# Attention as one loop over the tiles of all heads, with scores two tiles further ahead and the product with v two steps behind its transposition

## The chip, the cores and the metric

The kernel runs on one core of one Trainium2 chip. The metric is the device time of one execution in microseconds (us). Engines are named as in the profile: PE is TensorE's matmul, PEld its weight load, DVE is VectorE, ACT is ScalarE, POOL is GpSimd, SP is SyncE, which here only issues DMAs.

## The reference

Two sequences of 512 tokens with 1024 features go through one encoder layer. What matters here is the attention half:

```python
q = rms_norm(q, q_norm); k = rms_norm(k, k_norm)          # 8 heads of 96 = 64 + 32 rotary
y_att = block_attention(q, k, v)                          # softmax(q k^T * scale) v, v: 64 per head
h = h + jnp.concatenate([y_pool, y_att], axis=-1) @ w_o
u2 = rms_norm(h, ln2)
h = h + (jax.nn.silu(u2 @ w_gate) * (u2 @ w_up)) @ w_down
gate = jax.nn.sigmoid(rms_norm(h, ple_norm) @ w_ple_gate)
return h + gate * (p @ w_ple_proj)
```

Attention is bidirectional, without a mask. All arithmetic is in fp32; the kernel keeps an operand of a product as a high and a low part and makes each product of three matmuls (`mm3`).

## The kernel before, in words

A sequence has 512 tokens, that is 4 tiles of 128 rows (`NT = 4`). There are two sequences (`s0`, `s1`) of 8 heads each, so the attention has 16 heads and 64 tiles. For each tile of a head three things are done:

- `scores(q, h, t)`: three matmuls into a PSUM bank tagged `s` (three such banks), the row maximum on DVE (L517), its product with the row's scale (L518, one element per row), the exponential on ACT with the row's sum (L520), the reciprocal (L521) and the division by the sum, on DVE for t = 2 (L523) and on POOL else (L525). The result p lies in an SBUF slot tagged `F` (12 of them, shared with the scratch of the projections).
- `turned(q, h, j)`: four 128x128 transposes on PE (L531), one from each of the head's four p tiles, into a bank tagged `pt` (two of them), and a split into a high part (ACT, L128) and a low part (DVE, L131) in a slot tagged `PT` (four of them). So no `turned` of a head can start before all four p tiles of the head are there.
- `values(q, h, j)`: two matmuls (L543) that add into the head's bank `y`. There is one such bank. After the head's fourth `values`, `head_out` empties it with ACT (L553) and DVE (L554).

The loop `attention` goes over the heads, and in a head over its four tiles. While a head is turned, the scores of the next head are issued, one tile for each tile turned, so scores stand four tiles ahead. `values` follows its `turned` by one step, and the last one of a head comes at once after its last `turned`.

Other work is woven in. `must` holds one generator for each group of four heads: the projection of the next four heads (q, k, v, rotary part, normalisation, and the transposition of q and k of each head, lines 441 to 505). `RATE` says how many pieces of it are issued for each tile (2, 2, 1, 1). The scores of a head need its q and k to be there, so `run(block)` issues all the rest at the fourth head of a group. Once the block is used up in the third group, pieces of `more` are issued: the output projection `output(s0)`, which first splits eight tiles of attention and pooling results (`mixed`, tiles `ys`) and then goes through eight column tiles of `w_o` (matmuls `o<-ys`, addition L608). `output(s1)` follows after the attention.

The order of the text is not the order on the engines. The program is built with `tile.TileContext(nc, schedule_with_timeline_sim=True)`: a planner fixes each engine's order before the program runs, and takes work that it believes ready ahead of earlier work that it believes blocked. On the chip each engine then follows that order.

```python
BUFS = {"A": 20, "QK": 8, "V": 4, "PT": 4, "W": 8, "R": 2, "F": 12, "G": 4}
PSUM_BUFS = {"s": 3, "y": 1, "pt": 2, "g": 2}
"soft": "ppdp",
RATE = (2, 2, 1, 1)
attention([project(s0, 1, w1), chain(features(s1), project(s1, 1, w1)), again(), iter(())], o0, early)
run(o0)
```

Of the kernel before, what the change touches and what calls it, by code (L numbers as in the profile page):

```python
# [11 lines left out]
F32 = mybir.dt.float32  # L12
# [6 lines left out]
T = 512  # L19
NT = T // P  # L20
# [4 lines left out]
PAD = 8  # L25
# [13 lines left out]
HG = 4  # L39
# [47 lines left out]
def hybrid_layer(ctx: ExitStack, tc: tile.TileContext, a: dict, out: bass.AP):  # L87
# [6 lines left out]
    def nm(s):  # L94
        serial[0] += 1
        return f"{s}{serial[0]}"

    def sbuf(s, tag, shape, dt):
        return pool.tile([P] + shape, dt, tag=tag, name=nm(s), bufs=BUFS[tag])

    def At(s, tag="A", dt=F32R):
        return sbuf(s, tag, [2, T], dt)

    def Ft(s):
        return sbuf(s, "F", [T], F32)
# [6 lines left out]
    def eng(name, i=0):  # L112

        return nc.gpsimd if TURNS[name][i % len(TURNS[name])] == "p" else nc.vector

    def Ps(s, tag=None):
        if tag is None:
            tag = ALL_BANKS[turn[0] * 3 % 8]
            turn[0] += 1
        return psum.tile([P, T], F32, tag=tag, name=nm(s), bufs=PSUM_BUFS[tag])  # L120

    def col(s, n=16, bufs=8):
        return pool.tile([P, n], F32, tag=f"c{n}", name=nm(s), bufs=bufs)

    def split(hi, lo, src, hi_eng="act", lo_eng=nc.vector):

        if hi_eng == "act":
            nc.scalar.activation(hi, src, AF.Copy)  # L128
        else:
            nc.vector.tensor_copy(hi, src)  # L130
        lo_eng.tensor_tensor(lo, src, hi.bitcast(F32), op=ALU.subtract)  # L131
# [21 lines left out]
    def mm3(ps, lhs, rhs, first, last, more=False):  # L153

        nc.tensor.matmul(ps, lhs[0], rhs[0], start=first, stop=False, skip_group_check=more)  # L155
        nc.tensor.matmul(ps, lhs[0], rhs[1], start=False, stop=False, skip_group_check=more)  # L156
        nc.tensor.matmul(ps, lhs[1], rhs[0], start=False, stop=last, skip_group_check=more)  # L157

    def act(t, sl=slice(0, T), rows=P):
        return t[:rows, 0, sl], t[:rows, 1, sl]  # L160
# [4 lines left out]
    def tok(t):  # L165
        return slice(t * P, (t + 1) * P)
# [74 lines left out]
    s0, s1 = seqs  # L241
# [269 lines left out]
    def scores(q, h, t):  # L511
        qT, kT, rq, _, hh = q.heads[h]
        ps = Ps("s", "s")
        mm3(ps, act(qT, tok(t), QK), act(kT, rows=QK), True, True)
        r = rq[:, t * HG + hh:t * HG + hh + 1]
        c = col("sm", 4, 12)
        nc.vector.tensor_reduce(c[:, 0:1], ps, axis=AX.X, op=ALU.max, negate=True)  # L517
        nc.vector.tensor_tensor(c[:, 1:2], c[:, 0:1], r, op=ALU.mult)  # L518
        p = Ft("p")
        nc.scalar.activation(p, ps, AF.Exp, scale=r, bias=c[:, 1:2], accum_out=c[:, 2:3])  # L520
        nc.vector.reciprocal(c[:, 3:4], c[:, 2:3])  # L521
        if eng("soft", t) is nc.vector:
            nc.vector.tensor_scalar(p, p, c[:, 3:4], None, op0=ALU.mult)  # L523
        else:
            nc.gpsimd.tensor_scalar(p, p, c[:, 3:4], 1.0, op0=ALU.mult, op1=ALU.mult)  # L525
        q.p[h].append(p)

    def turned(q, h, j):
        ps = Ps("pt", "pt")
        for t in range(NT):  # L530
            nc.tensor.transpose(ps[:, tok(t)], q.p[h][t][:, j * P:(j + 1) * P], ident)  # L531
        pt = At("pt", "PT")
        split(pt[:, 0, :], pt[:, 1, :], ps)
        q.pt[h].append(pt)

    def values(q, h, j):
        _, _, _, v, hh = q.heads[h]
        if j == 0:
            q.y[h] = Ps("y", "y")

        vv = v[j // 2][:, j % 2, hh].rearrange("p a d -> p (a d)")
        for i in range(2):
            nc.tensor.matmul(q.y[h], vv, q.pt[h][j][:, i, :], start=(j == 0 and i == 0), stop=(j == NT - 1 and i == 1))  # L543

    def head_out(q, h):
        if h % 4 == 0:
            q.ya4 = At("ya", dt=F32)
        y = q.ya4[:, h // 2 % 2, :]
        if h % 2 == 0:
            q.ya.append((NG + h // 2, y))  # L550
        o = h % 2 * VD
        f = Ft("yf")
        nc.scalar.activation(f[:VD, :], q.y[h][VD:, :], AF.Copy)  # L553
        nc.vector.tensor_tensor(y[o:o + VD, :], q.y[h][:VD, :], f[:VD, :], op=ALU.add)  # L554

    def attention(must, more, after):

        for q in seqs:
            q.p = {h: [] for h in range(H)}
            q.pt = {h: [] for h in range(H)}  # L560
            q.y, q.ya = {}, []
        heads = [(q, h) for q in seqs for h in q.order]
        for t in range(NT):
            scores(s0, 0, t)
        for n, (q, h) in enumerate(heads):
            block = must[n // HG]
            for i in range(NT):
                if h % HG == HG - 1 and i == 0:
                    run(block)
                if n + 1 < len(heads):  # L570
                    scores(*heads[n + 1], i)
                turned(q, h, i)
                if i:
                    values(q, h, i - 1)
                for _ in range(RATE[n // HG]):
                    if next(block, 0) is not None and n >= 2 * HG:
                        next(more, None)
            values(q, h, NT - 1)
            head_out(q, h)
            after(q, h)  # L580


    def mixed(q, i):
# [184 lines left out]
    def run(*gens):  # L768
        for g in gens:
            for _ in g:  # L770
                pass
# [14 lines left out]
    s0, s1 = seqs  # L786
# [2 lines left out]
            next(g, None)  # L789

    RATE = (2, 2, 1, 1)
    latents()
    pools = pooling()
    steps(pools, 1)
# [15 lines left out]
    def again():  # L810
        yield from project(s1, 0, head_weights(0))

    attention([project(s0, 1, w1), chain(features(s1), project(s1, 1, w1)), again(), iter(())], o0, early)
    run(o0)
    phase[0] = "raw2"
# [254 lines left out]
```

## Time and profile before

| | us |
|---|---|
| median of 3 runs (1205.45 to 1207.92) | 1206.1 |
| the profiled execution | 1203.58 |
| its span, from the first to the last instruction | 1201.6 |
| PE busy in the span | 1131.3 |
| DVE busy | 927.1 |
| ACT busy | 591.2 |
| POOL busy | 195.6 |

The profiled execution is one execution of its own; its span leaves out 2.0 us before the first and after the last instruction. Busy time is time in which an engine executes; PE's is modelled from the matmuls' sizes. The granted clock of PE is given as a share of its full speed. The attention lies between 155 us, where the first scores start, and 381 us, where the last head's result is written.

### The profile page before, as it was taken

To read this page: it belongs to the slowest core of one execution; us is meant where nothing else is said; L and a number is where in the kernel's file an instruction comes from. 1 tells how busy PE (TensorE), PEld (TensorE's weight loads), DVE (VectorE), ACT (ScalarE), POOL (GpSimd) and SP (SyncE) were. 2 spreads that over 40 slices of the span, in tenths; PEclk is the share of its full clock that TensorE was granted. 3 is DMA by queue.
4 is the path that set the end of the run, shared out by engine and by line. 5 is a ranking of instruction groups with operands and counts; after the bars stand their busy time and mean duration, and the time that the engine had idled before them with its cause. 6 is when DMAs were issued, how large, how long until landed. Compare 5 with 4: busy or idle time off the path is not lost.

```text
span 1201.6 us, 15110 instructions
## 1 busy us (share of the span) xinstructions
PE 1131.3 (94%) x5232; PEld 936.6 (78%) x5232; DVE 927.1 (77%) x1738; ACT 591.2 (49%) x1135; POOL 195.6 (16%) x191
## 2 busy tenths in 40 slices
PE   7999979897999989999999999999669999999897
PEld 7998757785888867888888888888558888887775
DVE  7387799999684789988776877768547776896798
ACT  7154478777563536555444545455212222345553
POOL 3543562755330310000000000000000000001200
PEclk9999999997999989999999999999979999999999
DMA  6211100111242521644425444356896675526036
GB/s 216 69 56 58 36 1 1 53 36 53 88 142 88 167 79 55 226 176 158 163 91 185 175 158 140 105 193 234 296 412 233 251 278 203 210 88 227 27 122 220
DMA packets 53644, 173.26 MB, mean 144 GB/s; under 512 B 6208, under 2 KB 6976, under 8 KB 53568
## 3 DMA queue, kind: packets, MB, share of 16 engines
q1 hardware_dynamic: 53568, 172.30, 41.2%
q8 instruction: 41, 0.67, 0.2%
q14 instruction: 35, 0.29, 0.1%
HBM read 119.33 MB, written 52.95 MB: 143 GB/s over the span
## 4 chain that ended last, share of the span: by engine, by line
PE 73%; DVE 15%; DMA 4%; ACT 3%; issue 2%; POOL 1%; SPq 1%; DVEq 0%; POOLq 0%; ACTq 0%
PE a L156 7%; PE a L157 7%; PE a L155 7%; PE b L156 5%; PE b L155 5%; PE b L157 5%; PE d L157 3%; PE d L155 3%; PE d L156 3%; PE o L155 2%; PE o L156 2%; PE o L157 2%; PE c L155 2%; PE c L157 2%; PE c L156 2%
## 5 line engine op out<-in xcount | busy, mean ns | idle before, releaser
L128 ACT ACTIVATE w<-s 128x512 fp32r<-128x512 f32 (+2 forms) x168 | 97.1, 579 | 170.2 <-PE b L157 63.2
L156 PE MATMUL a<-u,w 128*128 128x512 f32 x444 | 173.5, 391 | 0.2 <-POOL u L131 0.2
L155 PE MATMUL a<-u,w 128*128 128x512 f32 x444 | 171.3, 391 | 1.5 <-ACT w L128 0.8
L157 PE MATMUL a<-u,w 128*128 128x512 f32 x444 | 171.2, 391 | 0.7 <-DVE w L131 0.7
L128 ACT ACTIVATE w<-raw 128x512 fp32r<-128x512 f32 (+2 forms) x126 | 70.9, 578 | 156.5 <-PE a L157 96.2
L155 PE MATMUL b<-u,w 128*128 128x512 f32 x296 | 117.1, 397 | 19.5 <-DMA u<-opT 19.5
L185 POOL TENSOR_TENSOR r<-base,neghalf 128x4 f32<-128x4 f32 x6 | 6.9, 1149 | 714.8 <-DVE base L194 714.3
L131 DVE TENSOR_TENSOR w<-s,w 128x512 fp32r<-128x512 f32 (+2 forms) x168 | 105.0, 628 | 22.7 <-ACT w L128 22.0
L156 PE MATMUL b<-u,w 128*128 128x512 f32 x296 | 117.3, 397 | 4.0 <-DVE u L131 4.0
L157 PE MATMUL b<-u,w 128*128 128x512 f32 x296 | 117.3, 396 | 1.1 <-DVE w L131 1.1
L155 PEld LDWEIGHTS a<-u,w 128*128 128x128 f32 x444 | 83.7, 189 | 20.0 <-ACT u L128 1.5
L157 PEld LDWEIGHTS a<-u,w 128*128 128x128 f32 x444 | 83.7, 188 | 18.9 <-DVE w L131 1.5
L156 PEld LDWEIGHTS a<-u,w 128*128 128x128 f32 x444 | 83.7, 188 | 18.0 <-POOL u L131 0.7
L131 DVE TENSOR_TENSOR w<-raw,w 128x512 fp32r<-128x512 f32 (+2 forms) x126 | 79.4, 642 | 23.5 <-ACT w L128 23.5
L155 PEld LDWEIGHTS b<-u,w 128*128 128x128 f32 x296 | 56.8, 192 | 32.7 <-DMA u<-opT 19.9
L156 PEld LDWEIGHTS b<-u,w 128*128 128x128 f32 x296 | 56.6, 191 | 17.0 <-DVE u L131 5.3
L157 PEld LDWEIGHTS b<-u,w 128*128 128x128 f32 x296 | 56.7, 191 | 13.5 <-DVE w L131 1.8
L155 PE MATMUL c<-u,w 128*128 128x512 f32 x148 | 58.7, 400 | 4.9 <-DVE x L727 4.9
L926 DVE TENSOR_TENSOR h<-h,a 128x512 f32<-128x512 f32 x64 | 42.4, 687 | 26.1 <-PE a L157 23.3
L641 DVE TENSOR_TENSOR s<-raw 128x512 f32<-128x512 f32 (+2 forms) x42 | 26.4, 628 | 43.1 <-DMA raw<-in_w_down 15.2
L157 PE MATMUL c<-u,w 128*128 128x512 f32 x148 | 58.6, 396 | 0.0
L156 PE MATMUL c<-u,w 128*128 128x512 f32 x148 | 58.6, 396 | 0.0
(234 smaller groups left out, 2844.7 us busy)
## 6 DMA issues: line engine op xcount, KB each, us to landing
opT<-st SPq DMA_DIRECT2D x44, 512.0 KB, 4.5
u<-opT SPq DMA_DIRECT2D x44, 512.0 KB, 7.7
opB<-st SPq DMA_DIRECT2D x33, 512.0 KB, 3.7
u<-opB SPq DMA_DIRECT2D x33, 512.0 KB, 9.9
raw<-in_w_gate SPq DMA_DIRECT2D x24, 512.0 KB, 4.3
raw<-in_w_up SPq DMA_DIRECT2D x24, 512.0 KB, 3.6
raw<-in_w_down SPq DMA_DIRECT2D x24, 384.0 KB, 6.2
raw<-in_w_o SPq DMA_DIRECT2D x16, 512.0 KB, 3.6
```

The lines of the kernel that those rows point to most:

```text
L128: nc.scalar.activation(hi, src, AF.Copy)
L131: lo_eng.tensor_tensor(lo, src, hi.bitcast(F32), op=ALU.subtract)
L155: nc.tensor.matmul(ps, lhs[0], rhs[0], start=first, stop=False, skip_group_check=more)
L156: nc.tensor.matmul(ps, lhs[0], rhs[1], start=False, stop=False, skip_group_check=more)
L157: nc.tensor.matmul(ps, lhs[1], rhs[0], start=False, stop=last, skip_group_check=more)
L185: nc.gpsimd.tensor_tensor(r[:, :n], base, neghalf[:, :n], op=ALU.pow)
L641: eng("wadd", k).tensor_tensor(d, x, y, op=op)
L926: nc.vector.tensor_tensor(h, h, ps, op=ALU.add)
```

## The change

The two nested loops become one loop over 64 turns, and the scores are taken from a list of 64 tiles, also across the border of a head. Before the loop six tiles are scored (`NT + AHEAD_S`) in place of four; then one is scored in each turn. `values` follows its `turned` by two turns (`LAG_V`), also across the border of a head, and `head_out` and `after` follow the head's last `values`. The p tile of t = 3 lies in a slot tagged `G` (four of them, 528 elements) in place of `F`. If the next tile to be scored belongs to a head that has not been projected, the rest of the block is issued first; with six tiles ahead this comes at turn 10 of a group of 16 where it came at turn 12.

```diff
-        p = Ft("p")
+        p = sbuf("p", "G", [T + 2 * PAD], F32)[:, :T] if t == NT - 1 else Ft("p")
...
-        for t in range(NT):
-            scores(s0, 0, t)
-        for n, (q, h) in enumerate(heads):
-            block = must[n // HG]
-            for i in range(NT):
-                if h % HG == HG - 1 and i == 0:
-                    run(block)
-                if n + 1 < len(heads):
-                    scores(*heads[n + 1], i)
-                turned(q, h, i)
-                if i:
-                    values(q, h, i - 1)
-                for _ in range(RATE[n // HG]):
-                    if next(block, 0) is not None and n >= 2 * HG:
-                        next(more, None)
-            values(q, h, NT - 1)
-            head_out(q, h)
-            after(q, h)
+        tiles = [(q, h, t) for q, h in heads for t in range(NT)]
+        turns = [(q, h, j) for q, h in heads for j in range(NT)]
+        block = [None]
+
+        def more_scores():
+            if tiles:
+                if tiles[0][1] not in tiles[0][0].heads:
+                    run(block[0])
+                scores(*tiles.pop(0))
+
+        for _ in range(NT + AHEAD_S):
+            more_scores()
+        for n, (q, h, j) in enumerate(turns):
+            group = n // (NT * HG)
+            block[0] = must[group]
+            if h % HG == HG - 1 and j == 0:
+                run(block[0])
+            more_scores()
+            turned(q, h, j)
+            if n >= LAG_V:
+                values(*turns[n - LAG_V])
+                if turns[n - LAG_V][2] == NT - 1:
+                    head_out(*turns[n - LAG_V][:2])
+                    after(*turns[n - LAG_V][:2])
+            for _ in range(RATE[group]):
+                if next(block[0], 0) is not None and group >= 2:
+                    next(more, None)
+        for q, h, j in turns[-LAG_V:]:
+            values(q, h, j)
+        head_out(q, h)
+        after(q, h)
...
+    AHEAD_S, LAG_V = 2, 2
```

## Rows read from the trace of the kernel before

**Rows 1.** The page: its first line, the engines' busy time, and PE's granted clock in 40 equal slices of the span.

```profile
span 1201.6 us, 15110 instructions
PE 1131.3 (94%) x5232; PEld 936.6 (78%) x5232; DVE 927.1 (77%) x1738; ACT 591.2 (49%) x1135; POOL 195.6 (16%) x191
PEclk9999999997999989999999999999979999999999
```

**Rows 2.** Busy time of each engine (and its instructions) in three stretches: length, PE, PEld, DVE, ACT, POOL, granted clock, share of the DMA engines, GB/s.

```profile
155.00:298.00 143.00, 122.61 (x635) 96.97 (x636) 134.95 (x314) 109.52 (x239) 81.48 (x108) 0.94 0.11 30
298.00:381.00 83.00, 82.86 (x410) 68.12 (x409) 57.65 (x105) 46.22 (x85) 22.76 (x20) 1.00 0.33 108
381.00:400.00 19.00, 19.00 (x86) 15.73 (x85) 9.43 (x12) 7.38 (x10) 0.00 (x0) 1.00 0.45 144
```

**Rows 3.** What PE waited for between 155 and 298 us: line, releaser, total us, times, longest. These are all the rows of that answer.

```profile
PE qkt L503 <- DVE v L131: 6.9, 2, 4.3
PE s L155 <- ACT p L520: 6.1, 5, 2.9
PE y L543 <- DVE pt L131: 3.1, 5, 1.3
PE qkt L503 <- DVE qkT L136: 1.4, 2, 0.8
PE y L543 <- ACT pt L128: 1.2, 2, 0.6
PE pt L531 <- DVE pt L131: 0.7, 1, 0.7
PE qkt L503 <- DVE sm L518: 0.6, 2, 0.3
PE pt L531 <- DVE p L523: 0.5, 1, 0.5
```

**Rows 4.** The same for DVE between 155 and 298 us, the longest of its rows.

```profile
DVE ssqq L446 <- ACT sqq L445: 1.6, 3, 1.0
DVE sm L521 <- ACT p L520: 1.4, 5, 0.6
DVE ya L554 <- ACT yf L553: 1.3, 3, 0.6
```

**Rows 5.** Row maxima (L517, DVE, one for each tile scored) in three stretches; the count is behind the busy time.

```profile
155.00:168.60 13.60, 6.05 (x9) 1.00 0.00 1
168.60:207.00 38.40, 8.81 (x13) 1.00 0.00 1
207.00:262.30 55.30, 12.86 (x19) 0.97 0.11 29
```

**Rows 6.** Transposes of p (L531, PE and its weight loads, four for each tile turned) in the same stretches.

```profile
155.00:168.60 13.60, 1.59 (x8) 1.05 (x8) 1.00 0.00 1
168.60:207.00 38.40, 10.56 (x68) 8.59 (x69) 1.00 0.00 1
207.00:262.30 55.30, 9.63 (x60) 7.57 (x59) 0.97 0.11 29
```

**Rows 7.** Groups of instructions by line over the whole span: count, busy us, mean ns of one, idle time of the engine just before them and its releasers.

```profile
L520 ACT ACTIVATE p<-s,sm,rq 128x512 f32<-128x512 f32 x64 | 49.9, 780 | 15.3 <-DVE sm L518 15.0
L131 DVE TENSOR_TENSOR pt<-pt,pt 128x512 fp32r<-128x512 f32 x64 | 43.4, 681 | 4.6 <-ACT pt L128 4.5
L517 DVE TENSOR_REDUCE sm<-s 128x1 f32<-128x512 f32 x64 | 43.3, 681 | 2.8 <-PE s L157 2.4
L518 DVE TENSOR_TENSOR sm<-sm,rq 128x1 f32<-128x1 f32 x64 | 18.6, 294 | 0.2
L554 DVE TENSOR_TENSOR ya<-y,yf 64x512 f32<-64x512 f32 x16 | 10.9, 682 | 8.9 <-ACT yf L553 8.6
L553 ACT ACTIVATE yf<-y 64x512 f32<-64x512 f32 x16 | 9.5, 594 | 13.7 <-PE y L543 13.6
```

**Rows 8.** One line of the answer for the tile `sm`: durations of L518 in ns, shortest, median and longest, and the first and last start.

```profile
L518 DVE TENSOR_TENSOR sm<-sm,rq x64: 132/150/2091, 158.3 to 360.7; 128x1 f32<-128x1 f32 x64
```

**Rows 9.** Busy time of each engine in two short stretches, columns as in rows 2.

```profile
282.00:289.00 7.00, 2.58 (x7) 1.23 (x7) 7.00 (x12) 3.95 (x11) 3.99 (x3) 0.52 0.33 97
289.00:298.00 9.00, 8.35 (x32) 6.72 (x33) 8.44 (x22) 5.35 (x11) 4.50 (x5) 0.61 0.08 34
```

**Rows 10.** The chain that ended last, in order of time, between 286 and 300 us: start, us on the chain, what.

```profile
289.65 1.06 PE qkt L503 x4
...
291.14 0.43 PE s L156
...
291.99 0.85 PE y L543 x2
...
297.25 0.70 PE s L155 x3
...
298.18 0.44 PE pt L531 x4
```

**Rows 11.** Instructions of ACT and of POOL in order of time: start, us, what.

```profile
275.71 2.27 ACT L128 ACTIVATE ys<-yp 128x512 fp32r<-128x512 f32 x4
277.79 2.26 ACT L128 ACTIVATE ys<-ya 128x512 fp32r<-128x512 f32 x4
...
281.84 3.46 POOL L131 TENSOR_TENSOR ys<-ya,ys 128x512 fp32r<-128x512 f32 x2
```

## The prediction, made before the changed kernel ran

> **What bounds the kernel now.** I read the page first: PE is busy 94% of the span, DVE 77% [rows 1], so over the whole span this is a PE kernel. The change touches only the attention, so I then asked for busy times by stretch, and there the picture splits in two [rows 2]. From 155 to 298 us DVE is busy 134.95 of 143 us and PE 122.61: DVE is the bound and PE idles 20.4 us. From 298 to 400 us PE is busy 101.86 of 102 us and DVE 67.08: the output projection of the first sequence fills every gap of PE, and no order of instructions can gain anything there.
>
> The waits of PE in the first stretch say the same [rows 3]: PE waits for DVE results or for banks that DVE and ACT have not emptied. The two longest (4.3 and 2.9 us) lie together between 278 and 288 us. There PE is busy only 2.58 of 7 us while DVE is busy for all 7, and its clock falls to the lower level, 1.2 GHz: the granted clock is 0.52 and then 0.61 [rows 9]. Up to about 297 us the chain that ends last runs over PE at that level, with 0.43 us for a score matmul that takes 0.70 / 3 = 0.23 us afterwards [rows 10].
>
> So there are three sums that the change could touch: 8.05 us in which DVE idles in its own stretch (143 - 134.95), 20.4 us of idle PE in it, and the half-speed piece at its end.
>
> **What the change removes and adds.** No instruction: 64 scores, 256 transposes, 128 products with v, 16 emptied banks and the projections stay, with shapes as they are. The p tile of t = 3 in `G` has the same 128x512 elements, so 0 us; in return `F` holds at most 8 live p tiles as before (10 live ones less two in `G`). No DMA is added. Those that move are the loads for the output projection, which come two turns earlier; the second stretch has its DMA engines a third busy [rows 2], so they cost 0, and if that cover were gone the projection would start late in a stretch in which DVE is the bound anyhow.
>
> **What it moves: scores.** Each tile is scored two tiles earlier. The aim can only be that a head's four p tiles are ready when its first transposition comes. That run-ahead partly exists already: the planner does not keep the order of the text. By 168.6 us there are 9 row maxima and 8 transposes, that is 9 tiles scored and 2 turned; by 207 us 22 against 19; by 262.3 us 41 against 34 [rows 5, 6]. Scores thus stand 7, 3 and 7 tiles ahead, where the text says four or five. Where DVE is short of time, the lead shrinks; a higher place in the order does not make DVE faster, it only pushes something else back.
>
> What is pushed back can be priced. When the output projection may start (turn 10 of the third group, where it was turn 12), the same number of tiles has been scored, but two fewer have been turned and two or three fewer multiplied with v. DVE has then done 2 x 0.68 us of splits less [rows 7] and half an emptied bank, 0.34 us: 1.7 us. PE has 2 x 0.44 us of transposes [rows 10] and 2 x 0.46 us of products (two matmuls of 0.23) left over for the stretch in which it is the bound: 1.8 us. The stretch of DVE ends 1.7 us earlier and that of PE grows by 1.8 us: 0 within the reading.
>
> **What it moves: DVE's gaps.** The 8.05 us of idle DVE are waits for ACT's squares, for the exponential, for the emptying of `y` [rows 4]: short ones, in an order fixed beforehand, at places where the next tile's scores were not there yet. With two more tiles scored, DVE has independent row maxima to do in such gaps, unless one of the three `s` banks is missing. Bounds: 0 (a fixed order stays fixed, and the gaps only go elsewhere) to 8.05 us (all filled). I take a little under half, because some of the waits shown (the squares, 1.6 us) belong to the projection and not to the attention. That is the only term with a sign: -3.5 us.
>
> **What it moves: the product with v.** Two turns behind its transposition, PE does not wait for the low part that DVE writes; those waits are 3.1 + 1.2 us [rows 3]. In DVE's stretch PE's waits are covered by DVE, so they are worth 0 alone; if DVE were not the bound, 4.3 us would be the gain. What is late next is the one bank `y`. In the old text two turns lie between a head's last product and the next head's first; in the new one there is one.
>
> **Collisions.** L518 is a product of one element in each row. Its median is 0.150 us, its longest 2.091, its mean 0.294 [rows 7, 8]: 64 x 0.144 = 9.2 us go into stretched ones, and the long ones fall where POOL works. Nothing in the change alters how often this happens, only where: 0, with bounds of -9.2 (none left) and +9.2 us (twice as many). The Trainium skill, "SBUF — State Buffer", section "Who interferes with whom", says that a DVE instruction with two SBUF inputs and a POOL instruction that reads SBUF take a shared port one at a time, and that the order of issue decides who blocks; by that rule the trace agrees, and earlier scores would exchange some collisions for others.
>
> **Sum.** Added and removed 0, deferred work 0, DVE's gaps -3.5, the half-speed piece 0, collisions 0: the profiled execution of 1203.58 us would become 1200.1. The median of the runs is 1206.1, 2.5 us above that execution, and the same difference carried over gives 1202.6 us.
>
> **Rivals.**
>
> *Only the order on paper changes.* The planner already runs ahead by up to 7 tiles, DVE stays the bound with the same work, and its gaps move without closing. For it: the counts of rows 5 and 6, and the 0 of the deferred work. Against it: at 207 us the lead was down to three, less than a head. Time: 1206.1, within 0.2% (2.4 us, about what a measurement of this kernel can tell from no change).
>
> *The bank `y` stops PE (slower).* Emptying takes 0.594 us on ACT and 0.682 on DVE, and one more DVE instruction of 0.68 ahead of it: 1.96 us [rows 7]. One turn of PE is 0.70 + 0.44 = 1.14 us [rows 10]. So PE would be stopped 0.8 us at each of 15 head borders. In DVE's stretch that is hidden; in PE's stretch there are some four borders, 3.3 us, hence 1209.4 us; if it lay open at all fifteen, 12 us, 1218. It decides as soon as less than 0.8 us of other ready PE work stands between the two products. Against it: no wait of PE for L554 stands in rows 3, and an output projection lies beside these borders.
>
> *The stall at the end of DVE's stretch grows or comes twice (slower).* The splits `ys` for the output projection come in one burst, 4.5 us on ACT and 3.46 us on POOL for two of them [rows 11], while the last heads are projected. The three heads forced at turn 10 instead of one at turn 12 make this burst denser. One more such pause is 4.4 us of idle PE (7 - 2.58), of which some 4 us would reach the chain: 1210. The half-speed piece on the chain is 7.6 us (289.65 to 297.25), of which 3.8 are due to the clock. The Trainium skill, "TensorE: Matmul & The Clock Gate", section "HAM oscillation — how this bites in real kernels", states that PE's clock is throttled again after pauses, so that work after each pause starts at half speed; by that rule the trace agrees, and each further pause would cost again.
>
> *The stall goes away (faster than forecast).* PE has more score tiles done and one or two products in hand during the burst; if that keeps the clock up, 3.8 us more are gained: 1198.8.
>
> **How the numbers follow.** Chances: DVE's gaps half filled 0.34, the same with the stall gone 0.10, order on paper only 0.32, bank `y` 0.12, a larger stall or more collisions 0.12. Faster by over 0.2% (below 1203.7) is 0.34 + 0.10 = 0.44, the same 0.32, slower (above 1208.5) 0.24. The likeliest case's own range is 1200 to 1204, most of DVE's gaps to a third of them. The range for the time goes from 1196, all gaps filled (1206.1 - 8.05 = 1198) with part of the half-speed piece, to 1210, the larger stall and the bank's 3.3 us.
>
> **What would show it.** In the profile after: between 155 us and the end of DVE's stretch, DVE's idle time about 4 us instead of 8; the lead of scores over turned tiles two larger at 207 us; that stretch ends at about 294 us instead of 298; from there PE is full until 400. If the lead is not larger, the first rival holds. A wait of PE or its weight loads for L554 shows the bank. A granted clock below 1 at the end of the stretch shows that the stall stayed. I would be wrong if PE's full stretch had gaps, if the second half of the kernel, which is not touched, came out with another order, or if DVE's busy time itself changed by more than 3 us, since collisions would then decide.

## The result, and the profile after

The changed kernel takes 1214.69 us in the median of four runs (1213.45 to 1216.59), beside 1207.01 us for the kernel before (four runs, three of which gave the 1206.1 us known ahead of the prediction): a ratio of 1.0058, with a 95% interval of 1.0037 to 1.0079. It is slower, by 7.7 us between the medians and by 7.0 us by the ratio, where 1202.6 us and a gain had been predicted. The profiled execution is the slowest of the four, 1216.59 us.

The page of the changed kernel (its first line, busy times, granted clock in 40 slices), and two lines of each trace that frame the attention: the row maxima (first and last start behind the three durations) and the products of the output projection of the first sequence. After:

```profile
span 1214.8 us, 15098 instructions
PE 1135.0 (93%) x5232; PEld 937.3 (77%) x5232; DVE 924.4 (76%) x1738; ACT 589.8 (49%) x1135; POOL 198.0 (16%) x191
PEclk9999999988999998999999999999979999999999
```

```profile
L517 DVE TENSOR_REDUCE sm<-s x64: 660/678/693, 163.1 to 364.2; 128x1 f32<-128x512 f32 x64
```

```profile
L155 PE MATMUL o<-ys,wh x128: 388/390/791, 320.4 to 429.2; 128*128 128x512 f32 x128
```

Before:

```profile
L517 DVE TENSOR_REDUCE sm<-s x64: 661/678/692, 157.2 to 360.0; 128x1 f32<-128x512 f32 x64
```

```profile
L155 PE MATMUL o<-ys,wh x128: 387/390/791, 307.7 to 417.7; 128*128 128x512 f32 x128
```

The two spans differ by 13.2 us [rows 1], and these rows divide it. Up to the first row maximum the profiled execution of after lost 5.9 us (163.1 against 157.2); the change has not begun there, and the last section comes back to it. From the first row maximum to the last output product it lost 5.6 us (266.1 against 260.5). The rest of the kernel took 1.7 us more. Within the attention all of the loss lies ahead of the first output product, 157.3 us after the first row maximum instead of 150.5. From then on the two are alike: 108.8 and 110.0 us.

The three stretches of rows 2, moved by the 6 us by which the attention starts later (length, PE, PEld, DVE, ACT, POOL, granted clock, DMA share, GB/s):

```profile
161.00:304.00 143.00, 118.16 (x612) 93.11 (x613) 128.59 (x306) 106.22 (x234) 81.58 (x108) 0.94 0.10 30
304.00:387.00 83.00, 81.92 (x410) 67.26 (x409) 61.43 (x112) 48.59 (x89) 24.15 (x20) 1.00 0.32 102
387.00:406.00 19.00, 19.00 (x85) 15.76 (x84) 6.01 (x8) 5.50 (x8) 0.00 (x0) 1.00 0.35 111
```

In the same 143 us DVE idles 14.41 us, where it idled 8.05 [rows 2], and PE idles 24.8 where it idled 20.4. No engine has become clearly busier (POOL by 0.1 us). The stretch that DVE bounds is longer, and DVE stands still more often in it. What it waited for there (line, releaser, total us, times, longest):

```profile
DVE sm L521 <- ACT p L520: 5.6, 10, 1.6
DVE pt L131 <- ACT pt L128: 3.5, 2, 2.9
DVE sm L517 <- PE s L157: 2.4, 7, 0.5
DVE lat L136 <- ACT lat L135: 0.9, 2, 0.5
DVE ssqq L446 <- ACT sqq L445: 0.5, 2, 0.3
```

The first row was 1.4 us in five waits [rows 4], and two more were, before:

```profile
DVE sm L517 <- PE s L157: 1.0, 1, 1.0
DVE pt L131 <- ACT pt L128: 0.9, 3, 0.4
```

DVE's order now puts the reciprocal (L521) of a tile so near behind the same tile's maximum that the exponential is still running. One such place, in order of time on DVE (start, us, what, idle before it and releaser in brackets):

```profile
218.84 0.16 DVE L518 TENSOR_TENSOR sm<-sm,rq 128x1 f32<-128x1 f32 x1
220.00 0.16 DVE L521 RECIPROCAL sm<-sm 128x1 f32<-128x1 f32 x1 [1.00 <-ACT p L520]
220.57 0.75 DVE L136 SCALAR_TENSOR_TENSOR lat<-lt,gain,lat 128x512 fp32r<-128x512 f32 x1 [0.41 <-ACT lat L135]
```

The longest single wait, 2.9 us for the high part of a split (L128), begins at 248.5 us. Just ahead of it PE goes through five products with v at the lower clock, after a wait for the bank `y`, and only then through the transposes that the split needs:

```profile
245.85 2.50 PE L543 MATMUL y<-pt,v 128*128 128x512 f32 x5 [1.11 <-DVE ya L554]
```

PE's waits between 161 and 304 us:

```profile
PE pt L531 <- DVE pt L131: 7.3, 6, 4.5
PE y L543 <- ACT pt L128: 4.9, 1, 4.9
PE qkt L503 <- DVE qkT L136: 3.5, 5, 1.2
PE s L155 <- ACT p L520: 3.0, 4, 1.3
PE qkt L503 <- ACT yf L553: 2.5, 1, 2.5
PE y L543 <- DVE ya L554: 1.3, 2, 1.1
```

Against rows 3 the waits for the low part of a split (`pt`, L131) that the lag was to take from `values` are gone there, but its wait for the high part (L128) went from 1.2 to 4.9 us, and 7.3 us of waiting now stand at the transposes. The wait for the bank `y` (L554), which was in no row before, is there, with 1.3 us.

### The profile page after: what moved, and what is told of

Its sections match the earlier page's. It is cut to its first block, busy times and chain, and to the rows that moved or that the text cites. A ratio compares the mean times of both kernels' runs of the same rounds, so it can differ in the third digit from the quotient of the medians.

```text
span 1214.8 us, 15098 instructions
## 1 busy us (share of the span) xinstructions
PE 1135.0 (93%) x5232; PEld 937.3 (77%) x5232; DVE 924.4 (76%) x1738; ACT 589.8 (49%) x1135; POOL 198.0 (16%) x191
## 4 chain that ended last, share of the span: by engine, by line
PE 77%; DVE 13%; DMA 4%; issue 2%; ACT 2%; POOL 1%; SPq 1%; DVEq 0%; POOLq 0%; ACTq 0%
PE a L156 7%; PE a L157 7%; PE a L155 7%; PE b L156 5%; PE b L155 5%; PE b L157 5%; PE d L157 3%; PE d L156 2%; PE d L155 2%; PE o L155 2%; PE o L156 2%; PE o L157 2%; PE c L155 2%; PE c L157 2%; PE c L156 2%
## 5 line engine op out<-in xcount | busy, mean ns | idle before, releaser
L128 ACT ACTIVATE w<-s 128x512 fp32r<-128x512 f32 (+2 forms) x168 | 96.9, 579 | 177.1 <-PE b L157 74.0
L128 ACT ACTIVATE w<-raw 128x512 fp32r<-128x512 f32 (+2 forms) x126 | 70.6, 577 | 153.3 <-PE a L157 96.3
L131 DVE TENSOR_TENSOR w<-s,w 128x512 fp32r<-128x512 f32 (+2 forms) x168 | 104.9, 628 | 22.5 <-ACT w L128 21.9
L131 DVE TENSOR_TENSOR w<-raw,w 128x512 fp32r<-128x512 f32 (+2 forms) x126 | 79.4, 642 | 23.4 <-ACT w L128 23.4
L156 PEld LDWEIGHTS b<-u,w 128*128 128x128 f32 x296 | 56.6, 191 | 17.1 <-DVE u L131 5.2
L157 PEld LDWEIGHTS b<-u,w 128*128 128x128 f32 x296 | 56.5, 191 | 13.7 <-DVE w L131 2.0
L155 PE MATMUL c<-u,w 128*128 128x512 f32 x148 | 58.7, 400 | 5.5 <-DVE x L740 5.5
L940 DVE TENSOR_TENSOR h<-h,a 128x512 f32<-128x512 f32 x64 | 42.4, 685 | 23.8 <-PE a L157 21.0
L520 ACT ACTIVATE p<-s,sm,rq 128x512 f32<-128x512 f32 x64 | 49.5, 777 | 19.6 <-DVE sm L518 19.5
L157 PE MATMUL c<-u,w 128*128 128x512 f32 x148 | 58.7, 397 | 0.0
```

The costliest lines, as they stand in the source:

```text
L940: nc.vector.tensor_tensor(h, h, ps, op=ALU.add)
```

## The experiments

Three theories stood at the start. A: scores further ahead take DVE, ACT and PE from the projection of the next heads, whose end starts the output projection. B: the product two turns behind holds the bank `y`. C: the order that the planner makes scatters, and no part of the change is the cause; in the later expectations it is called S, and C there names the end of a head that is put off. All ratios are to runs of the kernel before on the same chip.

**The parts of the change.**

```diff
-    AHEAD_S, LAG_V = 2, 2
+    AHEAD_S, LAG_V = 0, 2          # e1_lag_only
+    AHEAD_S, LAG_V = 2, 1          # e2_scores_only
+    AHEAD_S, LAG_V = 0, 1          # e3_loop_only, and: p = Ft("p")
-    RATE = (2, 2, 1, 1)
+    RATE = (3, 3, 2, 1)            # e4_rate3, else as the changed kernel
```

> The changed kernel with scores four tiles ahead as before (AHEAD_S 0) and the product with v two turns behind (LAG_V 2). Theory A (the earlier scores take DVE, ACT and PE ahead of the projection of the next heads, whose pieces come 3 to 9 us later in the trace of after, and this opens gaps on DVE at the group borders): 1207, within 2.4 us of before; DVE idle in its stretch (first score to first output product) about 8 us, and that stretch about 152 us long. Theory B (the later product with v holds the bank y and the PT slots, and PE and DVE wait for them): 1214, DVE idle about 15 us, PE waiting for L554. Theory C (any other text order gives the planner another order, with no one cause): anywhere between 1203 and 1215.

> The changed kernel with scores two tiles further ahead (AHEAD_S 2) and the product with v one turn behind (LAG_V 1). Theory A: 1214, as after; DVE idle in its stretch about 15 us, projection pieces late by 3 to 9 us. Theory B: 1207, DVE idle about 8 us. Theory C: anywhere between 1203 and 1215. If the two parts add up, e1 and e2 lie above before by amounts whose sum is about 7.5.

> The one loop with AHEAD_S 0, LAG_V 1 and all p tiles in F: only the way of writing the loop is left of the change; the product with v of a head's last tile comes one turn later than before. Theories A and B: 1207, within 2.4 us of before. Theory C: off by more than 2.4 us either way.

> The changed kernel, but the projection is woven in faster: RATE (3, 3, 2, 1) in place of (2, 2, 1, 1), so its pieces stand ahead of the extra scores again. Theory A: most of the loss goes, 1207 to 1210, the projection's pieces are no later than before. Theory B: 1214, since the product with v still lags. Theory C: anywhere between 1203 and 1215.

Measured: the lag alone 1207.9 us (1.0032, 1.0018 to 1.0046), the scores alone 1213.39 (1.0068, 1.0055 to 1.0082), the loop alone 1209.67 (1.0039, 1.0027 to 1.0051), the higher rate 1222.21 (1.0145, 1.0132 to 1.0158). The scores looked like the cause and B fell, since the scores alone lost as much as the whole change. But the loop alone, which only moves a head's last product by one turn, lost 4.8 us where A and B both had at most 2.4. The run with the higher rate tells less than it was made for: more pieces in the third group also issue the output projection faster, so that in its trace it stands ahead of attention tiles that are not done: 126 us lie between its first and its last output product, where it was 110.

**Where the extra scores stand, and the end of a head.** `e5_block_ahead` issues the pieces of projection that are woven in two turns earlier (the rest of a block is still issued at turn 10), so that the extra scores are no longer ahead of it; `e6_lead_late` scores four tiles ahead of the loop and the two others at turns 8 and 9 (`AHEAD_S` is 0 in the prologue). `e7_lag_in_head` (0, 2) and `e8_scores_in_head` (2, 1) end a head in its last turn, as the kernel before does.

```diff
 # e5_block_ahead
+        block[0] = must[0]
         for k in range(NT + AHEAD_S):
             more_scores()
+            if k >= NT:
+                for _ in range(RATE[0]):
+                    next(block[0], 0)
...
-            group = n // (NT * HG)
+            group = min((n + 2) // (NT * HG), len(must) - 1)
 # e6_lead_late
             more_scores()
+            if n in (8, 9):
+                more_scores()
 # e7_lag_in_head, e8_scores_in_head
-            if n >= LAG_V:
-                values(*turns[n - LAG_V])
+            if j >= LAG_V:
+                values(q, h, j - LAG_V)
...
+            if j == NT - 1:
+                for i in range(NT - LAG_V, NT):
+                    values(q, h, i)
+                head_out(q, h)
+                after(q, h)
```

> As the changed kernel (scores two tiles further ahead, products two turns behind), but the projection of the next heads is issued two turns earlier too, its first four pieces among the two extra scores ahead of the loop. Theory A (the extra scores cost because they stand ahead of the projection that the output projection waits for): back to the level of the lag alone, 1206 to 1209 us; the reductions of the projection's first squares come 7 to 8 us after the first score instead of 10.3, and the stretch up to the first output product is about 154 us instead of 159. Theory D (a lead of six tiles costs by itself, wherever the projection stands): 1212 to 1216, DVE idle about 15 us. Theory S (any other text gives another order and the time scatters without a cause): anywhere from 1203 to 1215, with no tie to the projection's pieces.

> As the changed kernel, but four scores ahead of the loop, and the two extra ones only at turns 8 and 9, when the first block of projection is issued. Theory A: the first block is not late, but the second and the third are, so some two thirds of the loss stays: 1210 to 1212 us; if only the start matters, 1206 to 1209. Theory D (the lead itself): 1211 to 1215, since the lead of six holds for 54 of 64 turns. Theory S: anywhere from 1203 to 1215.

> No extra scores; the product follows its transposition by two turns, but the last two products of a head and its emptying stand at the end of the head's last turn, as in the kernel before. The p tile of t = 3 lies in G. Theory C (what cost 0.3% in all forms of the one loop is the end of a head put off past the next head's first transposition): as the kernel before, 1203 to 1206 us. If the lag or the slots in G cost by themselves: 1208 to 1211. Theory S: anywhere from 1203 to 1215.

> Scores two tiles further ahead, product one turn behind, and a head's last product and its emptying at the end of its last turn, as in the kernel before: the extra scores alone, without the part that all forms of the one loop shared. If the two parts add (A for the scores, C for the end of the head): 1208 to 1210 us, that is 3 to 5 above the kernel before; first output product 4 to 6 us later after the first score. If the scores carry the whole loss of the changed kernel: 1212 to 1214. If they cost only together with the late end of a head: 1204 to 1206. Theory S: anywhere from 1203 to 1215.

Measured: 1205.0 us (1.0000, 0.9986 to 1.0014) with the projection two turns earlier, 1209.88 (1.0031, 1.0019 to 1.0042) with the lead built late, 1211.18 (1.0036, 1.0024 to 1.0048) and 1212.24 (1.0049, 1.0035 to 1.0063) with heads that end as before. The first of these is what A asks for, and had the experiments stopped here, A would have been told as shown. The third does not fit: no extra scores, no late end of a head, and yet 0.36% slower, with only the lag and the slot in `G` left to carry it.

**Projection earlier, and one slot.** `e10_slots_only` is the kernel before with the p tile of t = 3 in `G`. `e9_before_block_ahead` and `e12_before_block4` are the kernel before with the projection two and four turns earlier, `e11_block_ahead4` is the changed kernel with four.

```diff
 # e10_slots_only
-        p = Ft("p")
+        p = sbuf("p", "G", [T + 2 * PAD], F32)[:, :T] if t == NT - 1 else Ft("p")
 # e9_before_block_ahead: 2 turns; e11_block_ahead4, e12_before_block4: 4 turns
+            group = min((n + 4) // (NT * HG), len(must) - 1)
+            if (n + 4) % (NT * HG) == NT * (HG - 1):
+                run(must[group])
```

> The kernel before with one edit: the p tile of t = 3 lies in G and no longer in F. Order of the text, lead and lag are as before. Theory A (the time follows the end of the last projection block, which the text's order sets): as the kernel before, 1204 to 1207 us. Theory S (any edit makes the planner set another order, and orders other than that of the kernel before come out some 0.3% longer, as in the runs with the lag alone, the loop alone and the lag within the head): 1208 to 1211, with the last projection block ending 1 to 5 us later after the first score than the 151.2 us of the kernel before.

> The kernel before (lead of four, lag of one, end of a head in its last turn, all p in F), with every piece of the projection of the next heads two turns earlier, its first four pieces right after the first four scores. Theory A: the last projection block ends earlier, by up to two turns of some 4 us less what the tiles behind it lose; the time 1199 to 1204 us, and the output products start 2 to 6 us earlier after the first score than the 150.5 of the kernel before. Theory S: 1208 to 1211. If the projection is bound by DVE wherever it stands: 1204 to 1207.

> The changed kernel with the projection four turns earlier, where the run at 1205.0 us had it two turns earlier. Theory A: another step the same way, 1198 to 1204 us; output products start 143 to 147 us after the first score. If two turns only undid the two extra scores and the end of the block is set by DVE's work from there on: 1204 to 1207. Theory S: 1205 to 1211.

> The kernel before with the projection four turns earlier. Theory A: below the run with two turns, 1196 to 1203 us. If tiles of the attention then fail to be ready and PE waits for them behind the start of the output projection: 1204 to 1210, with idle PE between the first and the last output product, where every run so far but the one with the higher rate had none. Theory S: 1205 to 1211.

Measured: the slot alone 1211.65 us (1.0055, 1.0039 to 1.0072), almost the loss of the whole change. The kernel before with the projection earlier 1215.27 (1.0082, 1.0066 to 1.0097) by two turns and 1212.33 (1.0051, 1.0034 to 1.0067) by four; the changed kernel with four 1210.05 (1.0041, 1.0027 to 1.0055). A as a price of time falls: by it all three had to gain. What it says of the start holds in part: with four turns the first output product does come early (146.9 and 147.7 us after the first row maximum), and with two it did in the changed kernel (147.7) but not in the kernel before (154.6). But more of the attention is then left for the stretch in which PE is full, and PE waits there, for the low part of a weight that DVE splits (`wl`) and for a result of the attention (`ya`). In the run of the kernel before with four turns, from 307 to 430 us:

```profile
PE o L157 <- DVE wl L131: 1.8, 2, 1.3
PE o L155 <- DVE ya L554: 1.4, 1, 1.4
```

**Edits that change nothing but the order.** Each of the four transposes of a turned tile reads one of the head's four p tiles and fills its own quarter of the bank. The sequence in which they are written changes no dependence, size, slot, lead or lag, only which p tile is asked for first.

```diff
 def turned(q, h, j):
-        for t in range(NT):
+        for t in reversed(range(NT)):   # e14 (before), e16 (after), e18 (e5)
+        for t in (1, 0, 3, 2):          # e15 (before), e17 (after)
             nc.tensor.transpose(ps[:, tok(t)], q.p[h][t][:, j * P:(j + 1) * P], ident)
 # e13_after_no_slots: the changed kernel with
+        p = Ft("p")
```

The edit is small, but not quite neutral. That no transpose of a head can start before all four p tiles are there, as the section on the kernel before and the expectation below have it, is not so: in the kernel before PE takes the first two at 161.07 us, and two more wait until 162.92 us for the division of the third tile (L523). With the sequence reversed the planner has scores at the first of these places, 3.9 us after the first row maximum in both, and the first transposes come eight together at 168.10 us. The kernel before, and then with the sequence reversed:

```profile
161.07 0.38 PE L531 MATMUL pt<-cst,p 128*128 128x128 f32 x2
162.92 0.44 PE L531 MATMUL pt<-cst,p 128*128 128x128 f32 x2 [0.55 <-DVE p L523]
```

```profile
164.27 0.46 PE L155 MATMUL s<-qkT,qkT 96*128 96x512 f32 x1
168.10 1.74 PE L531 MATMUL pt<-cst,p 128*128 128x128 f32 x8
```

Up to 3.9 us after the first row maximum PE, DVE and ACT go through the same instructions in the same order in all twenty traces; from there on the planner's orders differ, in those of the edited sequences too. What the later start of three transposes can cost directly is, as an estimate, at most 3 x 0.11 us [rows 10] for each of 16 heads, 5.3 us if all of it lay open. That it decides is unlikely: the changed kernel came out no slower with the reversed sequence.

> The kernel before, with the four transposes of a turned tile written in the order t = 3, 2, 1, 0 in place of 0, 1, 2, 3. All four need the four p tiles of the head, so no dependence, size, slot, lead or lag changes. Theory A and every theory by which the position of scores, products or projection in the text decides: as the kernel before, 1203 to 1207 us. Theory S (the planner gives another order for any edit, and the kernel before has one of the shorter ones): 1207 to 1213 us.

> The kernel before, with the four transposes of a turned tile in the order t = 1, 0, 3, 2: a second edit that changes nothing but the planner's order. Theory A: 1203 to 1207 us. Theory S: 1207 to 1213 us, and another time than with the reversed order.

> The changed kernel with the four transposes in the order 3, 2, 1, 0. Theory A (the lead of scores costs): as the changed kernel, 1211 to 1215 us. Theory S: another draw, from 1204 to 1216 us, on average as far from the kernel before as its own neutral edits are.

> The changed kernel with its four transposes in the order 1, 0, 3, 2: the third order of the same text, beside 1.0058 as written and 1.0035 reversed; the kernel before has 1, 1.0049 and 1.0034 in the same three. Theory S: 1206 to 1216 us, and the means over three orders (0.28% for the kernel before) differ by less than 0.3%. If the lead of scores has a cost of its own above the scatter: above 1213, so that the mean of the changed kernel is over 0.5%.

> The changed kernel with all p tiles in F, as in the kernel before: lead and lag without the slots in G. If the slots in G carry the loss (alone they cost 0.55%): 1204 to 1207 us. Theory A (the lead of scores carries it): 1211 to 1215. Theory S: anywhere from 1204 to 1216. If F runs short, the exponential waits for a slot: above 1216.

> The changed kernel with the projection two turns earlier (level with the kernel before, 1.0000) with its transposes reversed. If that level comes from the earlier projection (theory A): 1203 to 1207 us. Theory S (it was a lucky order, as that of the kernel before): 1208 to 1213.

Measured, as ratios with intervals:

| order of the transposes | kernel before | changed kernel | changed, projection two turns earlier |
|---|---|---|---|
| 0, 1, 2, 3 | 1 | 1.0058 (1.0037 to 1.0079) | 1.0000 (0.9986 to 1.0014) |
| 3, 2, 1, 0 | 1.0049 (1.0037 to 1.0062) | 1.0035 (1.0022 to 1.0047) | 1.0033 (1.0018 to 1.0048) |
| 1, 0, 3, 2 | 1.0034 (1.0021 to 1.0047) | 1.0058 (1.0040 to 1.0077) | |

The changed kernel without the slots in `G` came out at 1.0030 (1.0018 to 1.0042). This settles most of it. The same kernel before, written with another sequence of four transposes, is slower by 0.49% (1212.51 us) or 0.34% (1210.92 us). Reversed, the changed kernel is ahead of the reversed kernel before by 0.14%; in pairs it is behind by 0.24%. Both differences are near the edge of what these runs can tell, but the sign of the change hangs on the sequence. And the one version that was level with the kernel before loses 0.33% by the same edit, so its level, too, belonged to one order.

The kernel before with reversed transposes, in its first 143 us of attention and the next 83 (columns as above), what DVE waited for in the 143, and its two framing lines:

```profile
158.00:301.00 143.00, 122.42 (x613) 96.83 (x614) 128.45 (x305) 106.39 (x233) 78.95 (x106) 0.92 0.10 30
301.00:384.00 83.00, 81.32 (x407) 66.49 (x405) 61.07 (x112) 48.62 (x90) 24.85 (x23) 1.00 0.30 100
```

```profile
DVE sm L521 <- ACT p L520: 4.8, 11, 1.2
DVE sm L517 <- PE s L157: 4.3, 7, 0.8
```

```profile
L517 DVE TENSOR_REDUCE sm<-s x64: 664/678/693, 160.3 to 369.1; 128x1 f32<-128x512 f32 x64
```

```profile
L155 PE MATMUL o<-ys,wh x128: 387/389/791, 316.7 to 426.7; 128*128 128x512 f32 x128
```

On DVE this is the picture of the changed kernel without the change: DVE busy 128.45 us (after 128.59, before 134.95 [rows 2]), the reciprocal waiting for the exponential 4.8 us, the row maximum for its scores 4.3 us, the first output product 156.4 us after the first row maximum, the last one 266.4 (after 157.3 and 266.1).

On PE it is another picture. From the first row maximum to the first output product, before, after and in the reversed kernel before (columns as above):

```profile
157.20:307.70 150.50, 130.08 (x684) 103.43 (x684) 142.52 (x332) 116.36 (x253) 82.86 (x110) 0.94 0.12 33
```

```profile
163.10:320.40 157.30, 131.40 (x690) 104.14 (x690) 142.14 (x341) 117.23 (x257) 83.66 (x111) 0.95 0.09 28
```

```profile
160.30:316.70 156.40, 134.43 (x682) 106.25 (x681) 140.00 (x332) 116.48 (x253) 82.47 (x110) 0.92 0.10 32
```

The changed kernel lost its time as idle PE, 25.9 us where it was 20.4. The reversed one idles only 22.0 us, but is busy 4.3 us longer with as much work, at a granted clock of 0.92 where it was 0.94: the lower level lasts 23.8 us there, 17.1 us before and 17.0 us after. So the two lose the same time in two ways, and the clock carries up to 3.4 us of it in one of them and none in the other.

All runs in one table. The two middle columns are us from the first row maximum to the first and the last output product; DVE's idle time is that of the 143 us from 2.2 us ahead of the first row maximum, which is 155 to 298 us in the kernel before.

| | ratio | first o | last o | DVE idle |
|---|---|---|---|---|
| before | 1 | 150.5 | 260.5 | 8.1 |
| after | 1.0058 | 157.3 | 266.1 | 14.4 |
| e1 lag only | 1.0032 | 152.2 | 262.1 | 10.6 |
| e2 scores only | 1.0068 | 157.9 | 266.6 | 14.2 |
| e3 loop only | 1.0039 | 154.1 | 264.0 | 13.0 |
| e4 higher rate | 1.0145 | 151.1 | 277.1 | 13.2 |
| e5 projection 2 earlier | 1.0000 | 147.7 | 259.6 | 9.6 |
| e6 lead late | 1.0031 | 155.5 | 264.3 | 13.8 |
| e7 lag in head | 1.0036 | 155.8 | 265.7 | 14.1 |
| e8 scores in head | 1.0049 | 158.2 | 267.2 | 16.6 |
| e9 before, projection 2 earlier | 1.0082 | 154.6 | 269.9 | 18.9 |
| e10 slots only | 1.0055 | 155.9 | 265.9 | 15.5 |
| e11 projection 4 earlier | 1.0041 | 147.7 | 264.1 | 11.5 |
| e12 before, projection 4 earlier | 1.0051 | 146.9 | 268.1 | 12.4 |
| e13 after, no slots in G | 1.0030 | 154.4 | 265.1 | 16.4 |
| e14 before, reversed | 1.0049 | 156.4 | 266.4 | 14.5 |
| e15 before, pairs | 1.0034 | 154.4 | 265.2 | 13.3 |
| e16 after, reversed | 1.0035 | 155.2 | 264.6 | 13.5 |
| e17 after, pairs | 1.0058 | 158.8 | 267.8 | 15.5 |
| e18 e5, reversed | 1.0033 | 151.2 | 263.2 | 12.0 |

The last output product says where the time is: its distance from the first row maximum follows the measured time within 2.5 us in every row (0.0058 of 1206 is 7.0, against 5.6; 0.0082 is 9.9, against 9.4; 0.0145 is 17.5, against 16.6). In 17 of the 18 other orders with the old rate the time is 0.30 to 0.82% longer than that of the kernel before; one is level and none is shorter. DVE idles more in all of them; but since its work is the same in all, a longer stretch must show more idle DVE, so this says where the time went and not why. Where the projection stands as before, nearly all of the loss lies ahead of the first output product; in e9, e11 and e12 most of it or all lies behind.

## Why the prediction was wrong

**DVE's gaps (-3.5 us): the step that failed.** The 8.05 us of idle DVE were read as a reserve that more ready work could only fill, with bounds from 0 to 8.05, because "a fixed order stays fixed, and the gaps only go elsewhere". But the change does not keep the order and move the gaps; the planner makes a new one, and the waits in it are new. Measured is 14.41 us, a term of +6.3 instead of -3.5. PE's idle time from the first row maximum to the first output product grew by 5.5 us with it, from 20.4 to 25.9, close to the 5.6 us of the attention. The lower bound should have been a loss: the two other sequences of the kernel before opened 6.5 and 5.3 us of the same gaps. What had looked like slack was the closest packing of the twenty, 94% of the stretch. The rows also bore less than was read from them: the three of rows 4 make 4.3 of the 8.05 us, and only 1.0 us was a wait for scores, which is what the prediction took the gaps for.

**Only order on paper.** This rival had the right thought and a wrong price. It took a new order to be worth 0; the other sequences of the kernel before price one at +4.1 and +5.9 us.

**The lead.** The forecast that at the time of 207 us the scores would be two tiles further ahead came true, and helped nothing. Row maxima and transposes in the three stretches of rows 5 and 6, moved by 6 us (after):

```profile
161.00:174.60 13.60, 6.07 (x9) 1.00 0.00 1
174.60:213.00 38.40, 9.89 (x15) 1.00 0.00 1
213.00:268.30 55.30, 10.37 (x16) 0.94 0.09 29
```

```profile
161.00:174.60 13.60, 2.84 (x16) 1.97 (x16) 1.00 0.00 1
174.60:213.00 38.40, 9.28 (x60) 6.98 (x60) 1.00 0.00 1
213.00:268.30 55.30, 9.99 (x60) 7.78 (x58) 0.94 0.09 29
```

At the end of the three, 9, 24 and 40 tiles are scored and 4, 19 and 34 turned: a lead of 5, 5 and 6 where it was 7, 3 and 7. The waits that grew on DVE are those for a tile's own exponential (by 4.2 us), for the high part of a split (2.6) and for a tile's own scores (1.4). The larger lead at the one time was thus not followed by fewer of them.

**Deferred work (0).** The step said that as many tiles are scored when the output projection starts, two fewer turned and two or three fewer multiplied. In the traces 55 tiles are scored, 49 turned and 48 multiplied at the first output product, where it was 52, 48 and 48. DVE had as much to do ahead of it, 142.1 us from the first row maximum where it was 142.5, and not 1.7 us less; the first output product came 6.8 us later.

**Bank `y`.** The wait showed, twice in DVE's stretch, with 1.1 us at the longest, near the 0.8 us that the rival gave a border. In the changed kernel it stands just ahead of DVE's longest wait, and what it is worth there is not shown. It need not make the whole kernel slower: the version with the projection two turns earlier has more of it and is level with the kernel before. In that version, from 159 to 302 us:

```profile
PE y L543 <- DVE ya L554: 4.3, 3, 2.7
```

**Stall and collisions (0 each).** The stall at the end of DVE's stretch did not go away; it grew, where 0 was forecast. Around it, after (columns as above), and then PE's two pauses in it, before and after:

```profile
286.00:305.00 19.00, 9.58 (x48) 7.88 (x46) 18.26 (x38) 13.11 (x30) 14.90 (x13) 0.73 0.28 83
```

```profile
282.11 0.66 PE L155 MATMUL s<-qkT,qkT 96*128 96x512 f32 x1 [2.90 <-ACT p L520]
287.92 0.63 PE L503 MATMUL qkt<-cst,k 128*96 128x128 f32 x2 [4.30 <-DVE v L131]
```

```profile
294.26 0.59 PE L543 MATMUL y<-pt,v 128*128 128x512 f32 x1 [4.92 <-ACT pt L128]
299.35 1.08 PE L531 MATMUL pt<-cst,p 128*128 128x128 f32 x4 [4.50 <-DVE pt L131]
```

The two pauses make 9.4 us where they made 7.2, which is 2.2 of the 5.5 us by which PE's idle time grew; this is half of what the rival of a larger stall priced, 4.4 us. In the reversed kernel before and in the one with pairs they make 7.7 and 8.1 us. The lower level of the clock lasts 10.2 us at the stall and 6.8 us around 245 us, 17.0 together; before it was 13.7 and 3.4 us. The half-speed piece on the chain was read too long: 0.61 over the 9 us of rows 9 puts the lower level's end at 296.0 us and not at 297.25, which makes 3.2 us of the 3.8. The mean of L518 went from 0.294 us [rows 7] to 0.312, which is 64 x 0.018 = 1.2 us. A long one beside a POOL instruction, first from DVE's timeline, then from POOL's:

```profile
239.59 2.11 DVE L518 TENSOR_TENSOR sm<-sm,rq 128x1 f32<-128x1 f32 x1
```

```profile
239.34 2.35 POOL L131 TENSOR_TENSOR wl<-raw,wh 128x1024 fp32r<-128x1024 f32 x1
```

The two overlap from 239.59 to 241.69 us. The Trainium skill, "SBUF — State Buffer", section "Who interferes with whom", has a DVE instruction with two SBUF inputs contend with a POOL instruction that reads SBUF; by that rule the trace agrees again. It would explain the length of this instruction. Of the loss it carries little by its length alone, since all of L518 has grown by only 1.2 us.

**The full stretch of PE** held: 81.92 us busy of 83 and 19.00 of 19.

**What is open.** Shown is that 17 of 18 other orders cost this kernel 0.3 to 0.8%, two of them with nothing changed but the sequence of four transposes, and that in the changed kernel the loss lies ahead of the first output product, beside 6.3 us more of waits on DVE. Not shown is which wait starts it; in the reversed kernel before the lower clock had a part. Not shown either is whether the lead or the lag has a price of its own. The mean over three sequences is 0.28% for the kernel before and 0.50% for the changed one; without the sequence as it was given it is 0.42% and 0.47%. With a scatter of 0.13 to 0.25% (the standard deviation of each three), three of each cannot tell a difference of 0.2%. The other runs say the same: with the projection and the rate as before, the seven versions with a lead of six (after, e2, e6, e8, e13, e16, e17) lose 0.47% in the mean, the six others with a lead of four (e1, e3, e7, e10, e14, e15) 0.41%. So the loss against the kernel before belongs mostly to that kernel's order, and how much of it, if any, to the lead stays open. Open too is why the order of the kernel before packs so closely. The changed kernel was not run with the order of the kernel before forced on it, engine by engine.

## What to carry to other kernels

Where a planner fixes the order, any edit is a new draw. Before a change of 0.5% is put down to its idea, run the old kernel with an edit that means nothing, such as another sequence of independent instructions (and check what it changes besides), and compare the change with that scatter. And a stretch in which the busiest engine is 94% full had more to lose by a new order here than to gain: the bounds of such a term need both signs. A single experiment that agrees with a theory (here the projection two turns earlier, level with the kernel before) should be repeated under a neutral edit before it is believed.

## What was not expected of the hardware

Ahead of the attention the change has moved nothing (the engines' orders are the same there), and yet the profiled executions differ there by up to 5.9 us. Busy time from 52 to 64 us (columns as above) before, after and in the kernel before with reversed transposes:

```profile
52.00:64.00 12.00, 11.72 (x81) 10.76 (x82) 1.75 (x10) 4.51 (x15) 1.64 (x2) 1.00 0.09 37
```

```profile
52.00:64.00 12.00, 9.26 (x43) 8.26 (x42) 1.91 (x9) 0.60 (x1) 3.09 (x3) 0.72 0.14 44
```

```profile
52.00:64.00 12.00, 11.67 (x57) 10.16 (x57) 1.31 (x7) 1.33 (x3) 1.01 (x1) 0.72 0.09 34
```

The granted clock is 1.00 in the first and 0.72 in the two others, with the lower level, 1.2 GHz, for 6.8 us. Half of 6.8 is 3.4 us, and the first row maximum of the reversed kernel comes at 160.3 us where it came at 157.2. All twenty traces sort by this. Ahead of the attention the lower level lasts 0 us in seven of them, with the first row maximum at 157.2 to 158.8 us; 3.4 us in six, at 158.8 to 160.1; and 6.8 us in seven, at 160.3 to 163.1. Between 50 and 56 us PE waits for `diag` (L201), 0.8 us in the execution of the kernel before, 2.7 in that of the changed one and 2.1 in the reversed one. The wait alone doesn't decide: with the loop alone (e3) it was 2.1 us too, and the clock stayed at 1.00. One execution's start is therefore no measure of a change; the comparison of stretches begins where the changed code begins.
